# Two layers of a hybrid trunk on one core: a planner's table of durations refitted, selector products replaced by lane shuffles, the inverse's products cut in 64-wide quarters, and the last layer's queries for half of the tokens

## The chip, the cores and the metric

The kernel runs on one core of one Trainium2 chip. The metric is the device time of one execution in microseconds. The chip's engines are named as in the profile: PE (matrix), PEld (its weight loads), DVE (vector), ACT (scalar), POOL (GpSimd), and SP, which here only issues transfers.

## What is computed

Two layers run over 256 latent tokens and 256 context tokens of width 1024. In each, a projection feeds three mixers (a long convolution, a gated delta rule in chunks, and attention); their outputs are gated, summed and projected, and a mixture of 16 experts with two of them chosen for each token follows. The last layer needs its output for the latent tokens alone. Cut to what matters here:

```python
def gated_delta_chunked(q, k, v, g, beta, s0):
    ...
    m = jnp.where(strict, jnp.einsum('nbhid,nbhjd->nbhij', kb, kc) * gamma, 0.0)
    t_inv = lax.linalg.triangular_solve(eye + m, ...)     # (I + M)^-1 of each chunk and head
    u = t_inv @ (vc * bc[..., None])
    w = t_inv @ (kb * jnp.exp(gc)[..., None])
    a_intra = jnp.einsum('nbhid,nbhjd->nbhij', qc, kc) * gamma
    ...
def trunk_layer(x, cx, ..., update_ctx):
    ...
    o_c, s_f, s_b = gdn_bidir(gdn_features(qkv_c, ...), s_zero, s_zero)   # context first: state only
    o_l, _, _ = gdn_bidir(gdn_features(qkv_l, ...), s_f, s_b)             # then the latents
```

In the last layer `update_ctx` is false, so the queries of the context tokens lead to no output.

## The kernel before

All fp32 products that carry the accuracy are made as three fp32r products of a high and a low part (`mm3`, `split_block`): for each block of weights ACT writes the rounded part (CAST) and DVE the rest (TENSOR_TENSOR to fp32r).

**Order.** The program is written once, instruction by instruction, by a planner, and every engine runs its own list in that order. Dense work is a list of *items* (`layer`, `run`): each loads weights by SP, splits them ahead of time (`prep_ahead`), runs 24 or so matmuls on PE and evicts. An item is named after its matrix: `k0`, `q0`, `v0`, `z0` for the delta rule's inputs, `uq` for attention's queries, `gatehy`, `gatemla`, `gategdn` and `proj...` for gates and branch projections, `woutt` for the output projection, `up` and `down` for experts. Beside them run *streams*, which are Python generators: `gdn_pair` for two heads of the delta rule, `attend`, `hy_conv`, `filters`, `route` and others. After every piece of an item (6 or 12 matmuls) `tick` asks which stream is ready, and writes that stream's next step into the lists. "Ready" is the word of the class `Plan` (`enter`, line 252): it keeps a clock for each engine and adds a duration for each instruction from a table of formulas. Nothing of it runs on the chip; it only fixes the order. Where a step stands too early in PE's list, everything behind it waits.

**The delta rule's inverse.** `gdn_system` (line 1056) handles two heads, two directions and two chunks at once, eight 128x128 lower triangles. It is called for the context (base 2) and for the latents (base 0), for two head pairs and two layers: 8 calls, here called systems. In a system, the eight 16x16 blocks on each diagonal are packed in a tile `X16` and inverted by back substitution on DVE (15 steps of a multiply and a reduce). Each step needs one row of every block on all 16 partitions of the block. Before, 16 products with a 0/1 matrix `rsel` spread these rows (PE), and four copies by ACT evict them into `B`. Then blocks of 16 are merged to 32 and 32 to 64: for n = 16 and 32 and both directions, N times U, a masked copy (COPY_PREDICATED on DVE) into V, then T times V and V times T, and two copies by ACT back to U and T. Each of these is four products of 128x128 by 128x128. A last 64-wide step makes the two results, which `gdn_scan` uses.

**Memory.** Work tiles come from 45 pages of 4 KB a partition (`NPAGE`, `Arena`), and `rsel` takes 8 KB a partition (`late_setup`).

**Around the output projection**, `rows` (called in `woutt00` of layer 0 and `woutt02` of layer 1) issues transfers of the residual rows and modulation rows from ACT's queue; the splits of later `woutt` weights that the planner put behind them on ACT come after them.

Of the kernel before, what the change touches and what calls it, by code (L numbers as in the profile page):

```python
# [17 lines left out]
F32 = mybir.dt.float32  # L18
# [4 lines left out]
AF = mybir.ActivationFunctionType  # L23
OP = mybir.AluOpType
# [6 lines left out]
L = 2  # L31
# [3 lines left out]
C_HY, C_QKV, C_Z, C_AB, C_CQ, C_CKV, C_KR, C_GATE = 0, 1536, 3072, 3584, 3600, 4368, 4624, 4656  # L35
# [1 line left out]
FF = 512  # L37
CAP = (128, 96)
BIG = 1 << 20
NPAGE = 45  # L40


def _constants():
# [183 lines left out]
class Plan:  # L227
# [4 lines left out]

    def __init__(self):
        self.clk = dict.fromkeys(("tensor", "vector", "scalar", "gpsimd", "sync"), 0.0)
        self.dma = self.hw = 0.0
# [18 lines left out]
    def enter(self, eng, op, a, k):  # L254
# [4 lines left out]
        outs, ins = aps[:1], aps[1:]  # L259
# [3 lines left out]
        t = self.clk[eng]  # L263
        for q in ik:
            t = max(t, self.done.get(q, 0.0))
# [6 lines left out]
        if "dma" in op:  # L272
            byte = 4 * max(math.prod(aps[0].shape), 1)
            if op.startswith("indirect"):
                byte = 4 * min(math.prod(x.shape) for x in aps[:2])
            if eng == "gpsimd":
                self.clk[eng] = t + 1040
                t += 2000
            else:
                self.clk[eng] = t + 50  # L280
                self.hw = max(self.hw, t) + 450
                t = min(self.hw, t + 2000)
            self.dma = max(self.dma, t) + byte / 360
            end = min(self.dma, t + 8000 + byte / 360) + 2000
            if eng == "sync":
                self.clk[eng] = max(self.clk[eng], self.dma - 9000)
        else:
            if eng == "tensor":
                if op == "transpose":
                    c = 0.84 * max(64, size(outs[0]))  # L290
                else:
                    m, w = size(ins[0]), size(outs[0])
                    if ins[0].dtype == F32R:
                        c = 0.417 * w if w >= 256 else 0.84 * w
                    else:
                        c = 1.67 * max(w, m)
                        c = c / 4 if m <= 32 and w > 128 else c / 2 if m <= 64 else c
                if t > self.clk[eng] + 3000:
                    self.warm = t + 4000
                if t < self.warm:  # L300
                    c *= 2
            elif eng == "vector":
                fast = op in ("tensor_scalar", "tensor_copy") and not ps
                c = 70 + (0.52 if fast else 1.04) * n + (61 if op in ("tensor_scalar", "scalar_tensor_tensor") and len(aps) > (2 if op == "tensor_scalar" else 3) else 0)
            elif eng == "scalar":
                fn = a[2] if op == "activation" else None
                if fn in (AF.Sin, AF.Exp, AF.Tanh) and (fn == AF.Sin) != self.sin:
                    self.sin = not self.sin
                    t += 1280
                c = (51 if ps else 93) + 0.834 * n + 93 * (len(aps) - 2)  # L310
            else:
                c = 100 + {"tensor_tensor": 2.15, "memset": 0.77}.get(op, 3.4) * n
            end = t + c
            self.clk[eng] = end
            end += 200 if eng == "tensor" else 130
# [45 lines left out]
class Trunk:  # L361
# [456 lines left out]
    def gdn_item(self, l, kind, h):  # L818

        nc = self.nc  # L820
        t = 4 * "qkv".index(kind) + h

        def post(b):
            o, th = self.M.get(), self.M.get()
            self.conv(b, o.f(), l, "gdn_conv_w", t, 512)
            nc.scalar.activation(th.f(), o.f(), AF.Tanh, scale=0.5)
            nc.vector.scalar_tensor_tensor(o.f(), th.f(), 1.0, o.f(), op0=OP.add, op1=OP.mult)
            th.free()
            self.g_in[kind, h] = o
        return self.win(l, C_QKV + 128 * t, 512, post, f"{kind}{h}")  # L830

    def abkr_item(self, l):

# [96 lines left out]
    def gdn_pair(self, l, hp):  # L930
# [5 lines left out]
        nc = self.nc  # L936
# [8 lines left out]

        for kind in "kqv":
            bs = []
            yield max(self.plan.when(self.g_in[kind, h].f()) for h in heads)
# [95 lines left out]
    def gdn_system(self, l, hp, base, fm, tm, sys):  # L1044
# [51 lines left out]
        R = self.rsel  # L1096
# [12 lines left out]
        if want_o:  # L1109
            mI = self.c("maskI").rearrange("p (d x) -> p d x", d=2)  # L1110
            for d in range(2):
# [1 line left out]
            self.unbank(bQ)  # L1113
            g_.tensor_tensor(AT.f(), AT.f(), E.f(), op=OP.mult)
        E.free()
        Bv = [x.f().rearrange("p (k u j) -> p k u j", k=8, u=8) for x in B]
        for j in range(14, -1, -1):
            n = 16 - j
            if j >= 8:
# [24 lines left out]
            self.unbank(b)  # L1144
        X16.free()

        lm = self.c("lm").rearrange("p (n x) -> p n x", n=2).bitcast(U32)
        for i, n in enumerate((16, 32)):
            for d in range(2):
                yield self.plan.when(U[d].f())  # L1150
                b = self.bank()
                for u in range(4):
                    t_.matmul(b[:, 128 * u:128 * u + 128], N.f(128, 512 * d + 128 * u), U[d].f(128, 128 * u), start=True, stop=True)
                v.copy_predicated(u4(V[n, d].f()), m4(lm[:, i]), u4(b))
                self.unbank(b)
            for d in range(2):
                yield self.plan.when(V[n, d].f())
                b, b2 = self.bank(), self.bank()
                for u in range(4):
                    t_.matmul(b[:, 128 * u:128 * u + 128], T[d].f(128, 128 * u), V[n, d].f(128, 128 * u), start=True, stop=True)  # L1160
                for u in range(4):
                    t_.matmul(b2[:, 128 * u:128 * u + 128], V[n, d].f(128, 128 * u), T[d].f(128, 128 * u), start=True, stop=True)
# [1273 lines left out]
    def late_setup(self):  # L2436
# [7 lines left out]
        self.rsel = self.sb.tile([128, 16, 128], F32, name="rsel")  # L2444
        nc.scalar.dma_start(out=self.rsel.rearrange("p k x -> p (k x)"), in_=a["dft"][:, 2048:4096])
# [120 lines left out]
```

## Time and profile before

| | us |
|---|---|
| three timed runs | 2143.42, 2138.56, 2142.91 |
| median | 2142.91 |
| profiled execution, its own time | 2147.72 |
| its span, first to last instruction | 2146.0 |
| PE busy | 1919.7 (89%) |
| DVE, ACT, POOL busy | 1273.9, 872.5, 343.7 |

Times of the trace are from the span's start. Mixing of layer 0 takes some 50 to 785 us, its output projection and routing to 893, its experts to 1194; layer 1 mixes from 1248 to 1771, and its experts run from 1840 to 2109. A matmul of fp32 is recorded twice (two passes), one of fp32r once; since matmuls overlap, the spacing of many in a row tells their cost, not the mean length of one. Nearly all instructions carry line 210, the planner's recorder, so groups are told apart by tiles and shapes: `pg` is a page, `bank` a PSUM bank, `cst` a table of constants.

### The profile page before, as it was taken

The page shows a single profiled execution, that of the slowest core. Times are in us where ns is not written, and L with a number is a line of the kernel's source. Part 1 is how long each engine was busy: PE and PEld are TensorE (multiplying, and loading weights), DVE is VectorE, ACT ScalarE, POOL GpSimd, SP SyncE. Part 2 cuts the span into 40 slices and gives each one's busy share as a digit, 9 for nine tenths or more (in the row PEclk, how much of TensorE's full clock was granted, in tenths as well). Part 3 has the DMA queues.
Part 4 walks back from the last instruction along what each step waited for, and adds up shares of the span by engine and source line. Part 5 has one row for each costly group of instructions (what it writes and reads, how often), then busy time and mean ns, then how long its engine had stood idle before and what let it go on. Part 6 is the DMA issues. An engine that isn't in the chain of part 4 may idle for free. (4 is left out here: it accounts for less than half of the span.)

```text
span 2146.0 us, 31293 instructions
## 1 busy us (share of the span) xinstructions
PE 1919.7 (89%) x11901; PEld 1438.5 (67%) x11902; DVE 1273.9 (59%) x2487; ACT 872.5 (41%) x1445; POOL 343.7 (16%) x318
## 2 busy tenths in 40 slices
PE   4999999999999978799999399988999996899993
PEld 1777887777778857688777277877787884433330
DVE  3665757555466557899988576666766655311113
ACT  3442334444433423388778344433454342010101
POOL 1210222000133004311110211220011212110002
PEclk9999999999999998899999699999999997899996
DMA  9725223312533264699996647413214349799961
GB/s 332 228 89 175 67 57 94 89 50 79 157 99 82 94 242 174 230 362 383 381 359 218 201 176 258 116 40 89 70 54 118 109 140 370 251 382 390 386 264 67
DMA packets 295751, 403.62 MB, mean 188 GB/s; under 512 B 43956, under 2 KB 185786, under 8 KB 295464
## 3 DMA queue, kind: packets, MB, share of 16 engines
q1 hardware_dynamic: 271512, 360.38, 50.0%
q10 hardware_dynamic: 13040, 21.33, 2.8%
q0 software_dynamic: 11040, 19.81, 2.7%
q8 instruction: 96, 1.57, 0.3%
q14 instruction: 63, 0.52, 0.1%
HBM read 394.56 MB, written 23.20 MB: 195 GB/s over the span
## 5 line engine op out<-in xcount | busy, mean ns | idle before, releaser
L210 PE MATMUL bank<-pg,pg 128*128 128x512 f32 (+5 forms) x9958 | 1704.5, 407 | 66.3 <-ACT pg L210 36.5
L210 PEld LDWEIGHTS bank<-pg,pg 128*128 128x128 f32 (+3 forms) x9958 | 1252.0, 173 | 466.6 <-issue 202.5
L210 DVE TENSOR_TENSOR pg<-pg,pg 128x1024 fp32r<-128x1024 f32 (+12 forms) x698 | 607.7, 901 | 205.1 <-ACT pg L210 195.7
L210 ACT CAST pg<-pg 128x1024 fp32r<-128x1024 f32 (+3 forms) x460 | 429.0, 965 | 248.9 <-DVE pg L210 151.5
L210 ACT COPY pg<-bank 128x512 f32<-128x512 f32 (+4 forms) x382 | 185.2, 507 | 372.3 <-PE bank L210 341.6
L210 POOL TENSOR_TENSOR pg<-pg,pg 128x1024 f32<-128x1024 f32 (+3 forms) x77 | 134.7, 1754 | 494.1 <-DVE pg L210 291.6
L210 PE MATMUL bank<-cst,pg 128*128 128x128 f32 (+3 forms) x935 | 143.1, 290 | 78.3 <-DVE pg L210 48.8
L210 PEld LDWEIGHTS bank<-cst,pg 128*128 128x128 f32 (+1 forms) x935 | 118.4, 160 | 131.4 <-issue 55.1
L210 ACT ACTIVATE pg<-bank 128x512 f32<-128x512 f32 (+1 forms) x116 | 61.1, 534 | 196.7 <-PE bank L210 190.8
L210 ACT ACTIVATE pg<-pg 128x512 f32<-128x512 f32 (+4 forms) x71 | 50.0, 710 | 139.3 <-DVE pg L210 121.0
L210 POOL DMA_INDIRECT yd<-pg,t_vi x28 | 28.3, 1012 | 480.3 <-ACT pg L210 244.3
L210 DVE SCALAR_TENSOR_TENSOR pg<-bank,vec,pg 128x510 f32<-128x510 f32 (+3 forms) x112 | 75.4, 676 | 46.6 <-ACT pg L210 44.7
L210 DVE TENSOR_TENSOR pg<-bank,pg 128x512 fp32r<-128x512 f32 (+4 forms) x120 | 69.8, 597 | 50.5 <-ACT pg L210 34.7
L210 DVE SCALAR_TENSOR_TENSOR pg<-pg,bank 128x512 f32<-128x512 f32 (+1 forms) x92 | 54.0, 601 | 76.1 <-ACT pg L210 67.6
L210 POOL TENSOR_TENSOR pg<-pg 128x512 f32<-128x512 f32 (+1 forms) x18 | 18.5, 1034 | 458.6 <-ACT pg L210 272.6
L210 DVE COPY pg<-bank 128x512 f32<-128x512 f32 x24 | 16.6, 692 | 113.6 <-PE bank L210 111.6
L210 DVE TENSOR_TENSOR pg<-pg,bank 128x512 f32<-128x512 f32 (+1 forms) x44 | 27.0, 613 | 73.4 <-PE bank L210 71.0
L210 ACT ACTIVATE pg<-bank,vec 128x512 f32<-128x512 f32 (+3 forms) x64 | 42.2, 659 | 64.0 <-PE bank L210 57.0
L210 ACT CAST pg<-bank 128x512 fp32r<-128x512 f32 (+1 forms) x72 | 35.8, 521 | 74.7 <-PE bank L210 68.4
L210 ACT ACTIVATE pg<-bank,t_amx,t_asq 128x512 f32<-128x512 f32 (+1 forms) x48 | 34.0, 708 | 78.8 <-DVE t_amx L210 78.8
L210 PE MATMUL bank<-pg,sc 128*32 128x512 f32 x384 | 54.6, 627 | 1.0 <-DMA pg<-in_w_ada_dram 1.0
L210 DVE TENSOR_TENSOR pg<-bank,cst 32x256 f32<-32x256 f32 (+1 forms) x56 | 28.5, 518 | 29.2 <-PE bank L210 25.5
(250 smaller groups left out, 841.8 us busy)
## 6 DMA issues: line engine op xcount, KB each, us to landing
pg<-in_moe_w_dram SPq DMA_DIRECT2D x384, 512.0 KB
pg<-in_w_in_dram SPq DMA_DIRECT2D x120, 512.0 KB
pg<-in_w_ada_dram SPq DMA_DIRECT2D x96, 512.0 KB
pg<-in_w_out_dram SPq DMA_DIRECT2D x24, 512.0 KB
pg<-modd ACTq DMA_DIRECT2D x12, 512.0 KB
pg<-yd SPq DMA_DIRECT2D x12, 512.0 KB
pg<-in_mla_w_uq_dram SPq DMA_DIRECT2D x16, 288.0 KB
pg<-gcd POOLq DMA_DIRECT2D x16, 256.0 KB, 4.0
```

The source lines that it names most:

```text
L210: return f(*a, **k)
```

## The change

Four edits. (1) The formulas of `Plan.enter` get other numbers, and each issuing engine gets a transfer clock of its own. (2) The products with `rsel` and their copies go; 16 STREAM_SHUFFLE instructions on DVE spread the rows within groups of 32 partitions, row k over the k+1 columns that are used. `rsel` goes, and `NPAGE` rises to 47. (3) The three products of each merge step are made for the two 64x64 quarters on the diagonal alone, 8 calls of 64x64 by 64x64 where there were 4 of 128; masked copy and evictions are split by halves of the partitions. (4) In layer 1 the four `q` items work on 256 tokens where they had 512.

```diff
-            if eng == "gpsimd":
-                self.clk[eng] = t + 1040
-                t += 2000
-            else:
-                self.clk[eng] = t + 50
-                self.hw = max(self.hw, t) + 450
-                t = min(self.hw, t + 2000)
...
+            self.clk[eng] = t + {"sync": 50, "scalar": 330}.get(eng, 1040 if far else 700)
+            self.dma[eng] = max(self.dma.get(eng, 0.0), t + 2000) + byte / 385
...
-                        c = 0.417 * w if w >= 256 else 0.84 * w
+                        c = max(111, 14 + 0.417 * w)
...
+        nt = 512 if kind != "q" or l < L - 1 else 256
...
-        for q in range(4):
-            b = self.bank()
-            for k in range(4):
-                t_.matmul(b[:, 128 * k:128 * k + 128], R[:, 4 * q + k, :], X16.f(128, 256), start=True, stop=True)
-            nc.scalar.copy(B[q // 2].f(512, 512 * (q % 2)), b)
-            self.unbank(b)
+        for k in range(15, -1, -1):
+            v.stream_shuffle(Bv[k // 8][:, k % 8, :, :k + 1], C[:, :, :k + 1], [16 * (i // 16) + k for i in range(32)])
+            if k == 8:
+                yield
...
+        halves = (0, 64)
+        quad = lambda x, o: u4(x)[o:o + 64, :, o:o + 64]
...
+        def prod(b, A, a0, B, b0):
+            for u in range(4):
+                for o in halves:
+                    t_.matmul(b[o:o + 64, 128 * u + o:128 * u + o + 64], A.f(64, a0 + 128 * u + o)[o:o + 64], B.f(64, b0 + 128 * u + o)[o:o + 64], start=True, stop=True)
...
-                v.copy_predicated(u4(V[n, d].f()), m4(lm[:, i]), u4(b))
+                prod(b, N, 512 * d, U[d], 0)
+                for o in halves:
+                    v.copy_predicated(quad(V[n, d].f(), o), m4(lm[:, i])[o:o + 64, :, o:o + 64], quad(b, o))
...
-                nc.scalar.copy(U[d].f(), b)
-                nc.scalar.copy(T[d].f(), b2)
+                for o in halves:
+                    nc.scalar.copy(quad(U[d].f(), o), quad(b, o))
+                    nc.scalar.copy(quad(T[d].f(), o), quad(b2, o))
```

The counts of whole program: PE loses 128 products with `rsel`, 384 of 128x128 and 96 of 512 columns become 768 of 64x64 and 96 of 256; DVE gains 128 shuffles and 32 masked copies (32 become 64); ACT trades 96 copies of 128x512 for 128 of 64x4x64.

Most rows stand in another place than before. Three places matter later. The first is DVE's list in the last system of layer 1 (`pg_1740` is its X16, `pg_1744` and `pg_1745` its B). Before, PE had this part:

```order
L210 MATMUL bank_66<-pg_1641_12446,pg_1668_12827 128x128
L210 MATMUL bank_66<-pg_1637_12326,pg_1668_12827 128x128
L210 MATMUL bank_70<-pg_1700_13234,rsel 128x128 x4
L210 MATMUL bank_67<-pg_1700_13234,rsel 128x128 x4
L210 MATMUL bank_63<-pg_1700_13234,rsel 128x128 x4
L210 MATMUL bank_65<-pg_1700_13234,rsel 128x128 x4
L210 MATMUL bank_64<-pg_1725_13514,pg_1677_12972 128x128 x2
```

Now DVE has it:

```order
L210 STREAM_SHUFFLE pg_1744_14240<-pg_1740_14141 128x8x4
L210 STREAM_SHUFFLE pg_1744_14240<-pg_1740_14141 128x8x3
L210 STREAM_SHUFFLE pg_1744_14240<-pg_1740_14141 128x8x2
L210 STREAM_SHUFFLE pg_1744_14240<-pg_1740_14141 128x8
L210 TENSOR_TENSOR pg_1742_14147<-bank_63,cst_72 128x512 x2
L210 TENSOR_TENSOR pg_1740_14141<-pg_1740_14141,pg_1745_14241 128x8x2
L210 TENSOR_REDUCE pg_1740_14141<-pg_1740_14141 128x8
```

The spreading of rows left PE and ACT, and stands on DVE directly ahead of the substitution.

The second place is PE's list at the end of layer 1's mixing, where the gates of the delta rule (`gategdn`, 128x256) are the last dense items that need nothing of it. Before, the last 64-wide products of the last system stood between the first of these items:

```order
L210 MATMUL bank_68<-pg_1677_12972,pg_1728_13569 64x64 x4
L210 MATMUL bank_68<-pg_1745_13900,pg_1728_13569 64x64 x4
L210 MATMUL bank_70<-pg_1386_9807,pg_1752_13942 128x256 x2
L210 MATMUL bank_70<-pg_1386_9807,pg_1753_13943 128x256
L210 MATMUL bank_70<-pg_1389_9823,pg_1752_13942 128x256 x2
L210 MATMUL bank_70<-pg_1389_9823,pg_1753_13943 128x256
L210 MATMUL bank_70<-pg_1390_9832,pg_1752_13942 128x256 x2
L210 MATMUL bank_70<-pg_1390_9832,pg_1753_13943 128x256
L210 MATMUL bank_70<-pg_1391_9841,pg_1752_13942 128x256 x2
L210 MATMUL bank_70<-pg_1391_9841,pg_1753_13943 128x256
L210 MATMUL bank_67<-pg_1700_13234,pg_1505_10897 64x64 x4
L210 MATMUL bank_63<-pg_1675_12924,pg_1700_13234 64x64 x4
```

Now the merge of that system begins behind the last of them, `gategdn7`:

```order
L210 MATMUL bank_69<-pg_1394_10092,pg_1766_14471 128x256 x2
L210 MATMUL bank_69<-pg_1394_10092,pg_1767_14472 128x256
L210 MATMUL bank_69<-pg_1395_10101,pg_1766_14471 128x256 x2
L210 MATMUL bank_69<-pg_1395_10101,pg_1767_14472 128x256
L210 MATMUL bank_68<-cst_71,pg_1774_14572 128x128 x4
L210 MATMUL bank_70<-cst_71,pg_1775_14589 128x128 x4
L210 MATMUL bank_65<-pg_1775_14589,pg_1739_14132 64x64 x8
L210 MATMUL bank_67<-pg_1776_14590,pg_1739_14132 64x64 x8
L210 MATMUL bank_63<-pg_1776_14590,pg_1774_14572 64x64 x8
L210 MATMUL bank_64<-pg_1774_14572,pg_1776_14590 64x64 x8
```

From there to `projgdn0`, 160 calls of the system and of its scan follow each other with no dense item between them. Before, all eight `gategdn` items and half of `projmla3` lay between the same steps.

The third place is ACT's list ahead of `rows` in layer 0: the casts of 128x1024 are splits of `woutt` weights, those of 128x512 split merged outputs. Before, one stood there:

```order
L210 CAST pg_539_5799<-pg_518_5571 128x1024
L210 CAST pg_541_5805<-pg_366_3540 128x512
L210 CAST pg_542_5810<-pg_370_3617 128x512
L210 CAST pg_544_5841<-pg_379_3742 128x512
L210 CAST pg_545_5846<-pg_380_3771 128x512
L210 DMA pg_551_5859<-in_x_dram 128x1024
```

Now three do (and one more was made before these rows):

```order
L210 CAST pg_544_5979<-pg_517_5791 128x1024
L210 CAST pg_546_6009<-pg_351_3487 128x512
L210 CAST pg_547_6014<-pg_351_3487 128x512
L210 CAST pg_550_6033<-pg_518_5793 128x1024
L210 CAST pg_552_6051<-pg_363_3688 128x512
L210 CAST pg_553_6056<-pg_92_541 128x512
L210 CAST pg_554_6071<-pg_533_5927 128x1024
L210 CAST pg_556_6089<-pg_376_3876 128x512
L210 CAST pg_557_6094<-pg_363_3688 128x512
L210 DMA pg_560_6101<-in_x_dram 128x1024
```

So `woutt02` and `woutt03` are split before the transfers are issued, where only `woutt00` and `woutt01` were.

## Rows read from the trace of the kernel before

**Rows 1.** The page, busy time of PE.

```profile
PE 1919.7 (89%) x11901; PEld 1438.5 (67%) x11902; DVE 1273.9 (59%) x2487; ACT 872.5 (41%) x1445; POOL 343.7 (16%) x318
```

**Rows 2.** Windows: layer 0's and layer 1's mixing, the latter's end, its projection.

```profile
core 0: us, PE busy (x) PEld busy (x) DVE busy (x) ACT busy (x) POOL busy (x), PEclk, DMA share, GB/s
100.00:785.00 685.00, 675.69 (x3752) 540.87 (x3751) 411.05 (x887) 276.10 (x509) 99.77 (x102) 0.99 0.34 98
1254.00:1705.00 451.00, 411.98 (x2905) 359.21 (x2903) 302.12 (x713) 194.43 (x381) 66.05 (x74) 0.94 0.36 104
1704.00:1758.40 54.40, 49.52 (x429) 48.16 (x429) 28.86 (x58) 21.98 (x39) 10.77 (x10) 0.99 0.46 155
1771.00:1840.00 69.00, 44.16 (x196) 36.02 (x197) 40.56 (x114) 13.93 (x27) 19.35 (x11) 0.70 0.89 331
```

**Rows 3.** PE by shape, whole span: the selector products.

```profile
L210 PE MATMUL bank<-pg,rsel 128*128 128x128 f32 x256 | 34.3, 299 | 4.6 <-DVE pg L210 4.6
```

**Rows 4.** PE in order of time, 154 to 160 us: one system's selector products.

```profile
155.88 3.74 PE L210 MATMUL bank<-pg,rsel 128*128 128x128 f32 x32
```

**Rows 5.** PE by shape, 1709 to 1719.6 us: products of the inverse, last system.

```profile
L210 PE MATMUL bank<-pg,pg 128*128 128x128 f32 x80 | 9.5, 278 | 0.0
```

**Rows 6.** PE by shape, 213.3 to 214.4 us: eight calls in one array quarter.

```profile
L210 PE MATMUL bank<-pg,pg 64*64 64x64 f32 x16 | 1.1, 221 | 0.0
```

**Rows 7.** PE by shape, 219.7 to 220.6 us: eight such calls in two quarters.

```profile
L210 PE MATMUL bank<-pg 64*64 64x64 f32 x8 | 0.7, 224 | 0.0
L210 PE MATMUL bank<-pg,pg 64*64 64x64 f32 x8 | 0.7, 224 | 0.0
```

**Rows 8.** PE in order of time, 213 to 221 us: their end.

```profile
220.25 0.45 PE L210 MATMUL bank<-pg 64*64 64x64 f32 x5
220.63 0.62 PE L210 MATMUL bank<-pg,pg 128*128 128x256 f32 x3
```

**Rows 9.** PE in order of time, layer 1: items of 512 and 256.

```profile
1260.11 5.78 PE L210 MATMUL bank<-pg,pg 128*128 128x512 f32 x24
1281.84 5.93 PE L210 MATMUL bank<-pg,pg 128*128 128x256 f32 x48
```

**Rows 10.** DVE by shape, whole span: copies of two sizes, and the masked copy.

```profile
L210 DVE COPY pg<-pg 128x48 f32<-128x48 f32 x64 | 8.1, 193 | 0.1
L210 DVE COPY pg<-bank 128x512 f32<-128x512 f32 x24 | 16.6, 692 | 113.6 <-PE bank L210 111.6 <-DMA pg<-in_moe_w_dram 2.0
L210 DVE COPY_PREDICATED pg<-cst,bank 128x512 f32<-128x512 uint32 x32 | 22.8, 729 | 22.7 <-PE bank L210 22.6
```

**Rows 11.** ACT by shape, whole span: evictions of the two sizes.

```profile
L210 ACT COPY pg<-bank 128x512 f32<-128x512 f32 x220 | 126.6, 588 | 303.1 <-PE bank L210 288.0 <-issue 7.0 <-DVE pg L210 4.6
L210 ACT COPY pg<-bank 64x256 f32<-64x256 f32 x24 | 8.7, 366 | 12.6 <-PE bank L210 12.4
```

**Rows 12.** PE by shape, 1704 to 1757.6 us: end of layer 1's mixing.

```profile
L210 PE MATMUL bank<-pg,pg 128*128 128x256 f32 x216 | 28.1, 285 | 0.2 <-DVE pg L210 0.2
```

**Rows 13.** PE in order of time: where that stretch begins and ends.

```profile
1703.95 1.26 PE L210 MATMUL bank<-cst,pg 128*128 128x128 f32 x8 [1.67 <-DVE pg L210]
...
1757.61 1.11 PE L210 MATMUL bank<-cst,pg 128*128 128x128 f32 x4 [4.61 <-POOL pg L210]
```

**Rows 14.** DVE and POOL in order of time: the last steps before it.

```profile
1748.78 0.42 DVE L210 TENSOR_TENSOR pg<-pg,bank 128x256 f32<-128x256 f32 x1 [4.18 <-PE bank L210]
...
1755.69 1.87 POOL L210 TENSOR_TENSOR pg<-pg,t_ors 128x512 f32<-128x512 f32 x1 [3.66 <-DVE t_ors L210]
```

**Rows 15.** PE, then ACT, in order of time: layer 0's projection.

```profile
806.11 0.80 PE L210 MATMUL bank<-pg,pg 128*128 128x512 f32 x1 [15.47 <-ACT pg L210]
...
800.15 4.82 ACTq L210 DMA_DIRECT2D pg<-modd  x6
805.01 5.78 ACT L210 CAST pg<-pg 128x1024 fp32r<-128x1024 f32 x6 [11.17 <-DMA pg<-in_ctx_dram]
```

**Rows 16.** PE in order of time: layer 0's first gathered rows.

```profile
899.94 1.35 PE L210 MATMUL bank<-cst,pg 128*128 128x128 f32 x8 [2.08 <-DMA pg<-h2d,t_gi]
```

More of the change, by code (lines that the diff above doesn't have):

```diff
@@ L39 @@
 BIG = 1 << 20
-NPAGE = 45
+NPAGE = 47
 def _constants():
@@ L275, in enter @@
                 byte = 4 * min(math.prod(x.shape) for x in aps[:2])
-            if eng == "gpsimd":
-                self.clk[eng] = t + 1040
-                t += 2000
-            else:
-                self.clk[eng] = t + 50
-                self.hw = max(self.hw, t) + 450
-                t = min(self.hw, t + 2000)
-            self.dma = max(self.dma, t) + byte / 360
-            end = min(self.dma, t + 8000 + byte / 360) + 2000
+            far = op.startswith("indirect")
+            self.clk[eng] = t + {"sync": 50, "scalar": 330}.get(eng, 1040 if far else 700)
+            self.dma[eng] = max(self.dma.get(eng, 0.0), t + 2000) + byte / 385
+            end = self.dma[eng] + (2500 if far else 0)
             if eng == "sync":
-                self.clk[eng] = max(self.clk[eng], self.dma - 9000)
+                self.clk[eng] = max(self.clk[eng], end - 9000)
         else:
@@ L293, in enter @@
                     if ins[0].dtype == F32R:
-                        c = 0.417 * w if w >= 256 else 0.84 * w
-                    else:
-                        c = 1.67 * max(w, m)
-                        c = c / 4 if m <= 32 and w > 128 else c / 2 if m <= 64 else c
+                        c = max(111, 14 + 0.417 * w)
+                    elif m <= 32 and w > 128:
+                        c = 0.42 * w
+                    elif m <= 64:
+                        c = 0.84 * w if w > 64 else 74 if ins[0].shape[0] <= 64 else 116
+                    else:
+                        c = 2 * max(4 + 0.84 * m, 38 + 0.835 * w)
                 if t > self.clk[eng] + 3000:
@@ L821, in gdn_item @@
         t = 4 * "qkv".index(kind) + h
+        nt = 512 if kind != "q" or l < L - 1 else 256
         def post(b):
             o, th = self.M.get(), self.M.get()
-            self.conv(b, o.f(), l, "gdn_conv_w", t, 512)
-            nc.scalar.activation(th.f(), o.f(), AF.Tanh, scale=0.5)
-            nc.vector.scalar_tensor_tensor(o.f(), th.f(), 1.0, o.f(), op0=OP.add, op1=OP.mult)
+            self.conv(b[:, :nt], o.f(nt), l, "gdn_conv_w", t, nt)
+            nc.scalar.activation(th.f(nt), o.f(nt), AF.Tanh, scale=0.5)
+            nc.vector.scalar_tensor_tensor(o.f(nt), th.f(nt), 1.0, o.f(nt), op0=OP.add, op1=OP.mult)
             th.free()
             self.g_in[kind, h] = o
-        return self.win(l, C_QKV + 128 * t, 512, post, f"{kind}{h}")
+        return self.win(l, C_QKV + 128 * t, nt, post, f"{kind}{h}")
     def abkr_item(self, l):
@@ L947, in gdn_pair @@
             bs = []
-            yield max(self.plan.when(self.g_in[kind, h].f()) for h in heads)
+            yield max(self.plan.when(self.g_in[kind, h].f(128 * nq if kind == "q" else 512)) for h in heads)
             for j, h in enumerate(heads):
@@ L1102, in gdn_system @@
                 t_.matmul(bQ[:, 128 * i:128 * i + 128], fm["k", h].f()[:, tok(c)], fm["q", h].f()[:, tok(c)], start=True, stop=True)
[L1103 to L1108 removed]
+        Bv = [x.f().rearrange("p (k u j) -> p k u j", k=8, u=8) for x in B]
+        for k in range(15, -1, -1):
+            v.stream_shuffle(Bv[k // 8][:, k % 8, :, :k + 1], C[:, :, :k + 1], [16 * (i // 16) + k for i in range(32)])
+            if k == 8:
+                yield
         if want_o:
@@ L1115, in gdn_system @@
         E.free()
-        Bv = [x.f().rearrange("p (k u j) -> p k u j", k=8, u=8) for x in B]
         for j in range(14, -1, -1):
@@ L1158, in gdn_system @@
                 b, b2 = self.bank(), self.bank()
[L1159 to L1162, printed above, removed]
-                nc.scalar.copy(U[d].f(), b)
-                nc.scalar.copy(T[d].f(), b2)
+                prod(b, T[d], 0, V[n, d], 0)
+                prod(b2, V[n, d], 0, T[d], 0)
+                for o in halves:
+                    nc.scalar.copy(quad(U[d].f(), o), quad(b, o))
+                    nc.scalar.copy(quad(T[d].f(), o), quad(b2, o))
                 self.unbank(b)
```

11 lines of the change are left out of this document (3 added, 8 removed).

## Prediction

> **What bounds the kernel now.** I read the page first: PE is busy 89% of the span [rows 1]. Next the windows: in layer 0's mixing PE works 675.7 of 685 us, in layer 1's 412.0 of 451, at its end 49.5 of 54.4, while DVE stays under 70% and the transfers under half [rows 2]. So mixing is bound by PE, and work taken from PE there is time, as long as some other item stands behind it; what PE waits for is a chain of hand-overs where no item does. Only in the projection of layer 1 (44.2 of 69 us, DMA share 0.89, granted clock 0.70) do the transfers set the pace. Then PE by shape and in order of time, for the cost of each kind of call that the change touches; last PE's gaps, for the places where order matters.
>
> The sum is made against the profiled execution, 2147.72 us (span 2146.0 and 1.7 around it), 0.22% above the median 2142.91. The forecast takes the same difference off the median. What a measurement can tell from no change is 0.3%, or 6.4 us: 2136.5 to 2149.3.
>
> **Selector products.** 128 calls of 128x128 go. One system has 16, in 32 records over 3.74 us, the last of which runs on for some 0.2 us [rows 4]: 0.112 us for each record, 0.224 for a call. The group has 256 records, 8 systems [rows 3]. All stand in stretches where PE is the bound: -128 x 0.224 = **-28.7**.
>
> **Queries of layer 1.** An item of 24 matmuls with 512 columns takes 5.78 us; two items of 256 columns took 5.93, so 2.97 for one [rows 9]. Four items: 4 x (5.78 - 2.97) = **-11.2**.
>
> **Products of the inverse.** 384 calls of 128x128 at 0.224 (the stretch of 80 records, 9.5 us busy, gives 0.238 [rows 5]; I take the lower) are 86 us. In their place come 768 calls of 64x64. Eight in one quarter of the array are 16 records in 1.1 us, about 0.117 a call with the tail off [rows 6]; eight that alternate between two quarters take 0.7, some 0.06 a call [rows 7]. The change alternates the two diagonal quarters in its innermost loop, so I take 0.062: 47.6 us, -38.4. Against it speaks the change of shape: after the last 64-wide call starts at about 220.48, the next 128-wide one starts at 220.63, 0.15 later where the spacing was 0.06 [rows 8], so 0.09 each way. Runs of 64-wide calls rise from 16 to 39 in PE's list: 23 x 0.19 = +4.4. Together **-34**. [...]
>
> **The end of layer 1's mixing.** The stretch from the last system's transposes to the scan's last ones takes 53.7 us (1703.95 to 1757.61 [rows 13]), of which 28.1 are dense matmuls of 256 columns [rows 12]; PE then waits only 4.61 [rows 13], for the normalisation, which runs from DVE's 1748.78 over POOL's 1755.69 [rows 14]. In the new list nearly all dense items stand ahead of the merge, and the 160 calls after `gategdn7` have no cover. How long the chain is alone, no row shows. It can't be under 53.7 - 28.1 = 25.6 (the other PE work and the old waits), less the 34/8 = 4.2 saved above, nor over 53.7. In between: PE's own work 49.5 - 28.1 - 4.2 = 17; some fourteen hand-overs to DVE or ACT (transposes, twice masked copy and eviction, the 64-wide step, the scan's two chunks) at 0.7 (eviction 0.59, masked copy 0.73 [rows 10, 11]) = 10; and the 8.8 from 1748.78 to 1757.61. I take 36, nearer the lower end because it adds up the steps. PE idles 36 - 17 = 19 where it idled 4.6: **+15** (bounds +1 and +32).
>
> **Other systems.** Elsewhere the list has three runs of 40 to 64 calls of a system with no dense piece between (the first pair in both layers). Some 13 hand-overs of 0.7 to 1.2 us: **+12** (0, if order lets earlier work reach over, to 34, where the whole saving of the products is waited away).
>
> **Layer 0's end of mixing.** The scan's last transposes stand behind `gategdn7` now: between 0 and the 8.8 of the same chain [rows 14], **+3**.
>
> **Output projection.** In layer 0 PE waits 15.47 us at 806.11 for ACT, which first had to issue (4.82 at 800.15) and then waited 11.17 for a transfer before its next split [rows 15]. Two more `woutt` items are split ahead of those transfers, and PE has 2 x 2.9 us (an item's half of 12 matmuls with 512 columns, half of 5.78) that it can do meanwhile: -5.8; in layer 1 one more, with 256 columns, -1.5. **-7.3**. What is late next is the transfer itself; if it is also issued later, this is nothing.
>
> **Experts.** The first gathered rows come at 899.94 after 2.08 of waiting for them [rows 16]. They stand two pieces earlier in the new list, so the wait grows: **+3** (0 to 5.8, two pieces of 2.9).
>
> **Clock.** PE's granted clock is 0.99 where it is busy, 0.70 in the projection where it works 44 of 69 us [rows 2]. In the bare chain 17 us of work could cost up to twice that, 17; I take **+4**.
>
> **DVE, ACT, POOL.** 16 shuffles of 8 to 128 elements a system, 68 on average. No row has one. The nearest is the COPY of 128x48, 0.193 long and 8.1/64 = 0.127 apart; the copy of 512 elements from a bank takes 0.692 [rows 10]. I take 0.16, below 0.127 being unlikely and 0.69 the upper bound: 128 x 0.16 = 20 us over eight systems, 2.6 in each. It lies beside dense items (DVE is idle 40% of layer 0's mixing and 33% of layer 1's [rows 2]), while ACT loses 32 copies of 0.59: **0**. ACT's other trade, 96 copies of 0.59 for 128 of about 0.37 [rows 11], and the masked copies, 32 of 0.73 for 64 of about 0.4, are nothing either: ACT is 40% and 43% busy there [rows 2]. If the cover of dense items fails, as at layer 1's end, the shuffles of that one system are still done before it. Two pages more only loosen waits. [...]
>
> **Sum.** -28.7 - 11.2 - 34 + 15 + 12 + 3 - 7.3 + 3 + 4 = **-44**. The profile would be 2103.5, the median 2142.9 - 44 = **2099**.
>
> **Rivals.**
> A. *The spread becomes the wait* (slower). Each shuffle carries a selector and may cost more than a copy; the substitution can't start before them, the merge not before it, and DVE's list holds the splits of dense weights behind them. It decides where the extra DVE time has no cover: above 0.16 + 44/128 = 0.50 us a shuffle the gain is gone. At 0.69 the loss is 128 x 0.53 = 68: about **2167**. For it: the row of 0.69, and DVE at 67% in layer 1. Against: the small copies of 0.127. Chance 0.13.
> B. *The inverse is bound by its hand-overs*, not by PE: the 34 of the products are waited for instead, **2133**. For: each merge step has a masked copy and two evictions behind it, and now twice as many of them. Against: PE's 1.4% of idle in layer 0, where dense items fill every gap. Chance 0.14.
> C. *The quarters don't run side by side* (the change doesn't do what it says): 768 x 0.117 = 90 in place of 47.6, +42, **2141**. Rows 7 speak against it. Chance 0.06.
> D. *The refitted numbers also fill idle time elsewhere*: layer 1's mixing leaves 39 us idle on PE [rows 2]; half of it, -20, gives **2079**. For: almost every row moves, and 39 us is the largest idle sum in mixing. Against: the moved dense work at its end is covered in the sum already. Chance 0.19.
> The forecast's own case, 2085 to 2115, has 0.48.
>
> **How the numbers follow.** The range leaves out A and the far edge of D: it runs from 2065 (D with the tail at its lower bound, 2079 - 14) to 2145 (C, with the shape changes on top). Faster by over 0.3%: the forecast, D, two thirds of B: 0.76. Within: C and the rest of B: 0.11. Slower: A: 0.13.
>
> **What would show it.** The selector group is gone; 64x64 records spaced about 0.03 each in runs; `q` items of layer 1 at 3 us; PE's busy time down some 75 us, to about 1845. In the windows layer 0's mixing ends some 25 us earlier; the end of layer 1's mixing shows PE idle for about 19 us, with DVE and ACT as releasers and a lower granted clock. The gap at the output projection of layer 0 is near 10. Shuffles last 0.15 to 0.25 and PE waits for none. I am wrong if shuffles are above 0.5, if 64-wide calls are spaced 0.117, or if the idle time of mixing rises by over 50.

## Result and profile after

The changed kernel takes 2117.6 us (median of 4 runs, 2112.6 to 2123.5) where the one before takes 2143.2. The ratio is 0.9886, with a 95% interval of 0.9857 to 0.9916: 25 us faster, and some 19 us slower than the forecast of 2099. The profiled execution took 2112.6 with a span of 2110.9, so it is the fastest of its kernel, while that of before (2147.7) lies over its median; the two spans differ by 35 us, the medians by 25. The stages below add up to the 35, so they overstate the change by some 10 us, and no row tells in which stage. The page's line of busy time answers to [rows 1]: PE has 66 us less to do, and idles 31 us more.

```profile
PE 1853.4 (88%) x12413; PEld 1368.1 (65%) x12414; DVE 1296.4 (61%) x2775; ACT 855.6 (41%) x1477; POOL 338.4 (16%) x318
```

The view of windows, cut where the first matmul of a stage stands on PE (mixing of layer 0; its projection and routing; experts; the border; mixing of layer 1; projection and routing; experts), first for after:

```profile
core 0: us, PE busy (x) PEld busy (x) DVE busy (x) ACT busy (x) POOL busy (x), PEclk, DMA share, GB/s
50.00:781.10 731.10, 696.09 (x4202) 542.55 (x4201) 464.04 (x1112) 292.55 (x561) 114.58 (x114) 0.98 0.37 112
781.10:872.30 91.20, 70.60 (x372) 59.17 (x372) 69.98 (x158) 26.83 (x45) 39.44 (x19) 0.89 0.72 259
872.30:1162.80 290.50, 286.32 (x1343) 236.22 (x1339) 270.76 (x284) 233.75 (x285) 34.25 (x30) 0.99 0.87 325
1162.80:1218.00 55.20, 15.88 (x67) 10.84 (x66) 33.30 (x50) 20.20 (x27) 15.89 (x9) 0.66 0.93 290
1218.00:1727.60 509.60, 447.69 (x3702) 390.49 (x3702) 356.15 (x940) 219.20 (x450) 72.45 (x84) 0.93 0.40 114
1727.60:1796.70 69.10, 41.71 (x211) 34.43 (x213) 39.17 (x111) 12.57 (x25) 18.61 (x11) 0.73 0.89 330
1796.70:2074.00 277.30, 271.24 (x2461) 87.72 (x2450) 33.77 (x60) 27.67 (x47) 22.15 (x22) 0.99 0.84 311
```

and the same stages before (columns as above):

```profile
50.00:785.00 735.00, 722.92 (x3950) 579.85 (x3951) 444.35 (x964) 297.00 (x541) 112.30 (x114) 0.98 0.36 108
785.00:893.30 108.30, 74.56 (x373) 61.75 (x371) 77.78 (x164) 29.82 (x49) 41.92 (x19) 0.81 0.64 235
893.30:1194.30 301.00, 292.81 (x1341) 234.75 (x1337) 270.67 (x282) 236.50 (x284) 34.06 (x30) 0.99 0.87 318
1194.30:1248.40 54.10, 15.26 (x68) 10.22 (x67) 33.03 (x50) 20.21 (x27) 15.92 (x9) 0.68 0.94 295
1248.40:1771.40 523.00, 479.11 (x3444) 423.68 (x3444) 343.12 (x794) 223.85 (x432) 76.82 (x84) 0.95 0.37 110
1771.40:1840.20 68.80, 43.95 (x215) 35.82 (x214) 40.19 (x113) 13.93 (x27) 19.35 (x11) 0.70 0.89 330
1840.20:2109.00 268.80, 268.56 (x2455) 87.53 (x2443) 33.97 (x61) 27.60 (x47) 22.22 (x22) 1.00 0.87 323
```

| stage | before | after | difference | forecast |
|---|---|---|---|---|
| mixing, layer 0 | 735.0 | 731.1 | -3.9 | about -25 |
| projection and routing, layer 0 | 108.3 | 91.2 | -17.1 | -5.8 |
| experts, layer 0 | 301.0 | 290.5 | -10.5 | +3 |
| border | 54.1 | 55.2 | +1.1 | 0 |
| mixing, layer 1 | 523.0 | 509.6 | -13.4 | about -15 |
| projection and routing, layer 1 | 68.8 | 69.1 | +0.3 | -1.5 |
| experts, layer 1, with the end | 268.8 | 277.3 | +8.5 | 0 |

So the time came from other places than forecast. Layer 0's mixing, from which PE lost 27 us of work (722.9 to 696.1), gave 4: the rest became idle time. The projection and the experts of layer 0, whose work is the same, gave 28.

Two parts of that are plain in the rows. On PE in order of time, the waits of the two projections and of the first gathered rows of each layer are now:

```profile
797.86 0.79 PE L210 MATMUL bank<-pg,pg 128*128 128x512 f32 x1 [5.67 <-ACT pg L210]
...
878.15 1.92 PE L210 MATMUL bank<-cst,pg 128*128 128x128 f32 x8 [4.18 <-DMA pg<-h2d,t_gi]
...
1746.54 0.80 PE L210 MATMUL bank<-pg,pg 128*128 128x512 f32 x1 [11.88 <-ACT pg L210]
...
1804.67 1.97 PE L210 MATMUL bank<-cst,pg 128*128 128x128 f32 x8 [6.06 <-DMA pg<-h2d,t_gi]
```

The first answers to the 15.47 of [rows 15], the second to the 2.08 of [rows 16]. Layer 1's gathered rows cost 6.06, where PE waited for none before:

```profile
1850.61 1.09 PE L210 MATMUL bank<-cst,pg 128*128 128x128 f32 x8
```

The place in the list that was forecast at +3 in layer 0 exists twice, and the forecast priced one.

In the second part of layer 0's experts, PE by line, before (1050 to 1194 us) and after (1030 to 1163 us):

```profile
L210 PE MATMUL bank<-pg,pg 128*128 128x512 f32 x540 | 133.4, 400 | 6.0 <-DVE pg L210 5.0 <-ACT pg L210 0.9
```

```profile
L210 PE MATMUL bank<-pg,pg 128*128 128x512 f32 x543 | 127.9, 393 | 0.0
```

Splits on DVE and ACT were late there by 6.0 us, and are not now. The busy time of about as many calls also falls by 5.5 us, which no row explains. The refitted table alone makes these experts as short (below).

### The profile page after: what moved, and what is told of

Its sections match the earlier page's. It is cut to its first block, busy times and chain, and to the rows that moved or that the text cites. A ratio compares the mean times of both kernels' runs of the same rounds, so it can differ in the third digit from the quotient of the medians.

```text
span 2110.9 us, 32623 instructions
## 1 busy us (share of the span) xinstructions
PE 1853.4 (88%) x12413; PEld 1368.1 (65%) x12414; DVE 1296.4 (61%) x2775; ACT 855.6 (41%) x1477; POOL 338.4 (16%) x318
## 5 line engine op out<-in xcount | busy, mean ns | idle before, releaser
L210 PE MATMUL bank<-pg,pg 128*128 128x512 f32 (+7 forms) x10732 | 1663.8, 390 | 77.0 <-ACT pg L210 48.0
L210 PEld LDWEIGHTS bank<-pg,pg 128*128 128x128 f32 (+5 forms) x10732 | 1212.9, 167 | 476.8 <-issue 199.2
L210 DVE TENSOR_TENSOR pg<-pg,pg 128x1024 fp32r<-128x1024 f32 (+14 forms) x697 | 603.2, 897 | 169.3 <-ACT pg L210 158.8
L210 ACT COPY pg<-bank 128x512 f32<-128x512 f32 (+5 forms) x414 | 171.0, 444 | 346.0 <-PE bank L210 301.7
L210 PEld LDWEIGHTS bank<-cst,pg 128*128 128x128 f32 (+1 forms) x935 | 117.8, 159 | 156.7 <-issue 54.1
L210 POOL TENSOR_TENSOR pg<-pg,pg 128x512 f32<-128x512 f32 (+3 forms) x77 | 131.6, 1714 | 446.2 <-DVE pg L210 274.1
L210 DVE TENSOR_TENSOR pg<-bank,pg 128x512 fp32r<-128x512 f32 (+4 forms) x120 | 69.1, 596 | 30.7 <-ACT pg L210 23.5
L210 DVE TENSOR_REDUCE pg<-pg 128x128 f32<-128x1024 f32 (+15 forms) x128 | 43.1, 336 | 4.4
```

The source lines that it names most:

```text
L210: return f(*a, **k)
```

## Experiments

In all of them the kernel before, run beside them, took 2141 to 2143 us. Where a planner sets the order, an edit moves everything behind it; so the first set changes parts and lets the planner answer, and the second keeps every instruction at its place.

### Parts with the planner free

**The table alone.** Kernel before, with the new `Plan.enter`.

```diff
-            self.dma = max(self.dma, t) + byte / 360
+            self.dma[eng] = max(self.dma.get(eng, 0.0), t + 2000) + byte / 385
...
-                        c = 0.417 * w if w >= 256 else 0.84 * w
+                        c = max(111, 14 + 0.417 * w)
...
```

> The kernel before, with the refitted table of durations alone: no instruction is added or removed, only the order moves. If the gain of the change is the work taken from PE and the new order costs part of it (theory), this is 2135 to 2165, with the waits around layer 0's output projection and the long stretch of experts shorter, and more PE idle time in mixing. If the refit itself is where the gain comes from (rival), it is near the changed kernel: 2115 to 2125.

Measured: 2133.5, ratio 0.9961 (0.9947 to 0.9975), just under the theory's range and outside the rival's. Nothing is taken from PE, and 9 us are gained: layer 0's stage from `woutt00` to the experts falls from 108 to 91 us and its experts by about 10, as in the changed kernel, while mixing of both layers becomes longer (735 to 739, 523 to 529). So both gains come without any work taken from PE. The projection's is not the table's alone: in the three runs below that have the old table but another order (shuffles alone, quarters alone, all edits) that stage takes 91 to 93 us too, with PE's wait for ACT at 3.5 to 6.2 us for the 15.47, behind a mixing that is 18 to 42 us longer. The experts stay at 301 us in the first two of these runs and take 295 in the third.

**Shuffles alone** (old table, 45 pages).

```diff
-                t_.matmul(b[:, 128 * k:128 * k + 128], R[:, 4 * q + k, :], X16.f(128, 256), start=True, stop=True)
...
+            v.stream_shuffle(Bv[k // 8][:, k % 8, :, :k + 1], C[:, :, :k + 1], [16 * (i // 16) + k for i in range(32)])
...
```

> The kernel before, with the lane shuffles in place of the selector products alone (45 pages, old table). Theory: PE loses 128 x 0.224 = 28.7 us and DVE's shuffles are hidden: 2110 to 2120. Rival (the shuffles become the wait): no gain, 2140 or more.

Measured: 2154.3, ratio 1.0054 (1.0036 to 1.0072): slower by 12, as the rival had it.

**Quarter products alone**, with masked copies and evictions by halves.

```diff
-                    t_.matmul(b[:, 128 * u:128 * u + 128], N.f(128, 512 * d + 128 * u), U[d].f(128, 128 * u), start=True, stop=True)
+                prod(b, N, 512 * d, U[d], 0)
...
```

> The kernel before, with the 64-wide quarter products, masked copies and evictions alone. Theory: 34 us less on PE, 2105 to 2115. Rival (the merge is bound by its hand-overs): 2133 to 2143.

Measured: 2154.9, ratio 1.0061 (1.0044 to 1.0078): slower by 13, above both ranges.

**256-token queries alone.**

```diff
+        nt = 512 if kind != "q" or l < L - 1 else 256
```

> The kernel before, with the four query items of layer 1 on 256 tokens alone. Theory: 4 x 2.8 = 11 us less, 2130 to 2134. Rival (they cover something that is waited for anyway): 2140 or more.

Measured: 2148.1, ratio 1.0029 (1.0014 to 1.0044): slower by 6, as the rival had it.

**All edits with the old table** (47 pages).

```diff
-            self.dma[eng] = max(self.dma.get(eng, 0.0), t + 2000) + byte / 385
+            self.dma = max(self.dma, t) + byte / 360
...
```

> The changed kernel with the old table of durations (shuffles, quarters, 256 tokens and 47 pages stay). If the new order gives back part of what PE lost (theory), the old one keeps the sum of the parts better in mixing but has the long wait at layer 0's output projection: 2085 to 2115. If the refit is what gains (rival), 2125 to 2143.

Measured: 2172.3, ratio 1.0138 (1.0109 to 1.0167). Both theories' numbers are missed. Each edit that takes work from PE makes the kernel slower by itself under the old table, and together they do by 31. With the new table they give 2117.6. So the refit is worth 9 us to the old instructions and 55 to the new ones. That could be the order, or the edits' own cost, which these runs can't separate.

**Two pages less** in the changed kernel.

```diff
-NPAGE = 47
+NPAGE = 45
```

> The changed kernel with 45 pages. Layer 0's experts took 12 us less than before, which was not forecast. If the two pages do it (more weights under way), this is about 2130, with that stretch at 300 us again; if the order of the steps does it, 2112 to 2123 and 290 us.

Measured: 2131.9, ratio 0.9961 (0.9947 to 0.9975). The pages are worth 14 us, but not in the experts, which take as long as with 47: mixing does, 744 in place of 731 us in layer 0 and 522 in place of 510 in layer 1. I had costed them at nothing. Since the planner asks for free pages before it steps a stream, they move the order too.

### Parts with every instruction in its place

Here the planner goes on counting one form of the work, and the chip gets the other. Without this, the runs above can't be read.

**Wide products in the changed kernel.**

```diff
+                    self.plan.enter("tensor", "matmul", (b[o:o + 64, ...
...
+            self.plan.off = True
+                t_.matmul(b[:, 128 * u:128 * u + 128], A.f(128, a0 + 128 * u), B.f(128, b0 + 128 * u), start=True, stop=True)
+            self.plan.off = False
```

> The changed kernel, every instruction in the same place of every list, but with the merge's products 128 wide again (the planner still counts the 64-wide ones). If PE is the bound at the merges, 34 us more: 2147 to 2155. If the hand-overs bind there, the wider products lie in the waits: 2120 to 2130.

Measured: 2142.0, ratio 1.0000 (0.9988 to 1.0013): the quarters are worth 24 us in this order. It lies between the two expectations, nearer to PE as the bound. The page's line of busy time:

```profile
PE 1889.9 (88%) x11645; PEld 1409.8 (66%) x11646; DVE 1294.9 (60%) x2775; ACT 857.8 (40%) x1477; POOL 338.2 (16%) x318
```

PE has 36.5 us more to do than in the changed kernel (1853.4), and the kernel is 24 us longer, so some 12 of the work that the quarters save lie where PE would wait anyway. The masked copies and evictions are split in both kernels; what splitting costs is not in the 24.

**Each shuffle twice in the changed kernel.**

```diff
+            self.plan.off = True
+            v.stream_shuffle(Bv[k // 8][:, k % 8, :, :k + 1], C[:, :, :k + 1], [16 * (i // 16) + k for i in range(32)])
+            self.plan.off = False
```

> The changed kernel, same order, each lane shuffle issued twice: DVE gets 128 x 0.25 = 32 us more. If the shuffles are hidden, 2115 to 2123 as the changed kernel; if the shuffles are on the path, up to 2150, and what they cost now is of that size too.

Measured: 2142.6, ratio 1.0002 (0.9991 to 1.0014): 25 us slower, for 30 us more on DVE (1326.6 busy, 1296.4 in the changed kernel). The shuffles are not hidden.

**Shuffles in the order of before.** The planner counts the selector products and their copies, which aren't issued; the sixteen shuffles stand where they stood.

```diff
-                t_.matmul(b[:, 128 * k:128 * k + 128], R[:, 4 * q + k, :], X16.f(128, 256), start=True, stop=True)
+                self.plan.enter("tensor", "matmul", (b[:, 128 * k:128 * k + 128], R[:, 4 * q + k, :], X16.f(128, 256)), dict(start=True, stop=True))
...
+        self.plan.off = True
...
+            v.stream_shuffle(Bv[k // 8][:, k % 8, :, :k + 1], C[:, :, :k + 1], [16 * (i // 16) + k for i in range(32)])
+        self.plan.off = False
```

> The kernel before, with the planner still counting the selector products, so that every instruction keeps its place, and the shuffles issued where the products stood. With a new order the shuffles made the kernel 12 us slower. If the order did that (theory), the products' 28.7 us come off here: 2112 to 2125. If the shuffles themselves are on the path (rival), 2140 to 2155 again.

Measured: 2154.0, ratio 1.0054 (1.0035 to 1.0074). The theory that the order gives the gain back falls: with no instruction moved, the time is the same 2154 that the free planner made. The page's line:

```profile
PE 1895.7 (88%) x11645; PEld 1409.5 (66%) x11646; DVE 1300.7 (61%) x2743; ACT 855.7 (40%) x1413; POOL 344.1 (16%) x318
```

PE has 24 us less to do than before (1919.7; 28.7 by the spacing of the calls), DVE 27 more (1273.9), and the kernel takes 11 us more by the medians (the two profiled executions differ by 2.4 alone). So the shuffles and what they bring cost some 35 to 40 here.

One system shows where. PE in order of time, before, 590 to 626 us:

```profile
593.48 3.74 PE L210 MATMUL bank<-pg,rsel 128*128 128x128 f32 x32
...
616.59 0.66 PE L210 MATMUL bank<-cst,pg 128*128 128x128 f32 x4 [0.46 <-DVE pg L210]
```

and with the shuffles in the same order:

```profile
595.20 5.32 PE L210 MATMUL bank<-pg,pg 128*128 128x512 f32 x22 [0.53 <-DVE pg L210]
...
619.50 2.13 PE L210 MATMUL bank<-cst,pg 128*128 128x128 f32 x8 [5.58 <-DVE pg L210]
```

The selector's 3.74 us are gone, and the transposes behind the same three dense items, which started at 616.59 after a wait of 0.46, start at 619.50 after one of 5.58. DVE in order of time, the substitution's first steps and its last, before:

```profile
597.91 0.18 DVE L210 TENSOR_TENSOR pg<-pg,pg 128x16 f32<-128x16 f32 x1
...
598.32 2.35 DVE L210 TENSOR_TENSOR pg<-pg,pg 128x24 f32<-128x24 f32 x1
...
615.52 0.29 DVE L210 TENSOR_REDUCE pg<-pg 128x8 f32<-128x128 f32 x1
```

and with the shuffles:

```profile
600.91 0.17 DVE L210 TENSOR_TENSOR pg<-pg,pg 128x16 f32<-128x16 f32 x1
...
601.32 2.35 DVE L210 TENSOR_TENSOR pg<-pg,pg 128x24 f32<-128x24 f32 x1
...
618.43 0.29 DVE L210 TENSOR_REDUCE pg<-pg 128x8 f32<-128x128 f32 x1
```

The substitution takes 17.9 us before and 17.8 now, with under 1 us of idle time on DVE in either; it starts 3.0 us later. Of these, 2.4 are the sixteen shuffles ahead of it, and 0.6 is that DVE came to this system later (its last long reduce ahead of the shuffles starts at 589.15 before, at 589.72 now). So the gain of one system is taken back, with more, at its next step, because DVE has nothing to hide the shuffles behind. The multiply of 128x24 lasts 2.35 us in both, where it takes 0.20 alone (in the kernel before, at 248.47); it is looked at below.

**All edits in the order of before** (old table, 45 pages): quarters and 256 columns in the same way.

```diff
+            if self._plan.small:
+                a = tuple(half(x) for x in a)
             return f(*a, **k)
...
```

> The kernel before with all three edits in its own order: the planner counts the old instructions, the chip gets shuffles, quarter products and 256-token queries (old table, 45 pages). With the order left to the old table these edits gave 2172. Theory (the order gives the gain back): 2143 - 28.7 - 24 to 34 - 11 = 2070 to 2085. Rival (the work left PE, and what it covered is waited for in any order): 2125 to 2145.

Measured: 2137.5, ratio 0.9971 (0.9961 to 0.9982), in the rival's range. Against the run with shuffles alone, quarters and 256-token queries together are worth 16.5. The planner with the old table had made 2172 of the same edits, with two pages more: there the order did cost, some 35 us.

**All edits in the order that the new table makes for the old instructions** (45 pages): the kernel of the run above, with the diff of the table alone.

> The same on the order that the refitted table makes for the old instructions (45 pages); that order alone took 2133. Theory: 2060 to 2080, faster than both kernels. Rival: 2115 to 2135.

Measured: 2120.4, ratio 0.9902 (0.9878 to 0.9927): 13 us less than the same order with the old instructions. The rival's range, again.

### What is late on DVE

DVE in order of time in the changed kernel, 156 to 166 us: two of a system's shuffles, and the first steps of the substitution behind them.

```profile
158.91 0.01 DVE L210 LOAD_MASK_SELECT pg<-pg  x1
158.91 0.22 DVE L210 STREAM_SHUFFLE pg<-pg 128x64 f32<-128x64 f32 x1
...
159.05 0.23 DVE L210 STREAM_SHUFFLE pg<-pg 128x56 f32<-128x56 f32 x1
...
161.24 0.17 DVE L210 TENSOR_REDUCE pg<-pg 128x8 f32<-128x16 f32 x1
161.44 2.24 DVE L210 TENSOR_TENSOR pg<-pg,pg 128x24 f32<-128x24 f32 x1
163.72 0.18 DVE L210 TENSOR_REDUCE pg<-pg 128x8 f32<-128x24 f32 x1
163.93 0.21 DVE L210 TENSOR_TENSOR pg<-pg,pg 128x32 f32<-128x32 f32 x1
```

POOL at the same time:

```profile
161.23 2.40 POOL L210 TENSOR_TENSOR pg<-pg,pg 128x1024 f32<-128x1024 f32 x1 [0.81 <-DVE pg L210]
```

A shuffle follows the last by 0.14 here. Each has a LOAD_MASK_SELECT of 0.01 us ahead of it. The multiply of 128x24 takes 2.24 us, where its neighbour of 128x32 takes 0.21: it ends at 163.68, within 0.05 us of POOL's product of 128x1024, AT times E, which started just ahead of it at 161.23 and took 2.40. No row names POOL as what held it; that is read from the two ends. Six of the eight systems have such a product. Before, DVE waited for the selector's evictions while POOL made it: in three of the six the product fell into that wait nearly whole (the first multiply, 128x16, took 0.19, 0.27 and 0.44 us), in two it held the first multiply for part of its length (0.94 and 1.48 us), and in one, that of 598.32 above, it held the second for 2.35. With the shuffles in the same order all six are held for 2.2 to 2.35, some 8 us more in all. With the 19 of the shuffles this makes up the 27 by which DVE's busy time rose. The products with a bank as source and the shuffles, of which 24 ran beside POOL's products in the run of shuffles in the order of before, were not longer for it. In that run the seven shuffles from 157.43 on, beside POOL's product of 128x512 at 156.93, take 0.27 to 0.31 us, and the same seven from 597.31 on, beside none, 0.26 to 0.32; in the kernel before, the pair of products with a bank takes 1.28 at 157.39, beside POOL's product at 156.89, and 1.28 at 243.44, beside none.

The last run moves POOL's product, and the two mask products of DVE that it needs, ahead of the shuffles, in the kernel of 2120.4:

```diff
+            for d in range(2):
+                v.tensor_tensor(u4(AT.f(512, 512 * d)), u4(bQ), m4(mI[:, d]), op=OP.mult)
+            g_.tensor_tensor(AT.f(), AT.f(), E.f(), op=OP.mult)
...
         for k in range(15, -1, -1):
...
-            g_.tensor_tensor(AT.f(), AT.f(), E.f(), op=OP.mult)
```

> The previous kernel on the refitted order (2120), with one thing moved: the two mask products of the intra-chunk matrix (DVE, from a PSUM bank) and POOL's product of 128x1024 behind them stand ahead of the sixteen shuffles and no longer behind them; everything else keeps its place. In the runs so far DVE's second multiply of the substitution (128x24, 0.20 us alone) lasts 2.2 to 2.35 in the six systems in which POOL's product runs beside it, and no shuffle that ran beside POOL's work was longer. Theory (that stall holds up the transposes): six times 2.1 us come off DVE, the six multiplies are 0.2 again, and the kernel is 5 to 13 us faster: 2107 to 2115. Rival (POOL then stalls another instruction, or the masks wait for PE): 2117 to 2125.

Measured: 2103.0 (2098.5 to 2109.3), ratio 0.9810 (0.9785 to 0.9834). That is 17 us less than without the move, more than expected, and faster than both kernels. By the two ratios the move is worth 12 to 27 us, and the two profiled executions differ by 11, so the stall that was known, six times 2.1 us, may be all of it. The same system without the move, DVE, POOL and PE in order of time:

```profile
596.68 2.34 DVE L220 TENSOR_TENSOR pg<-pg,pg 128x24 f32<-128x24 f32 x1
...
596.56 2.40 POOL L220 TENSOR_TENSOR pg<-pg,pg 128x1024 f32<-128x1024 f32 x1 [2.68 <-issue]
...
612.17 1.72 PE L220 MATMUL bank<-cst,pg 128*128 128x128 f32 x8 [4.82 <-DVE pg L220]
```

and with it:

```profile
592.57 0.29 DVE L220 STREAM_SHUFFLE pg<-pg 128x96 f32<-128x96 f32 x1
...
594.18 0.34 DVE L220 TENSOR_TENSOR pg<-pg,pg 128x16 f32<-128x16 f32 x1
...
594.76 0.21 DVE L220 TENSOR_TENSOR pg<-pg,pg 128x24 f32<-128x24 f32 x1
...
592.07 2.41 POOL L220 TENSOR_TENSOR pg<-pg,pg 128x1024 f32<-128x1024 f32 x1 [0.26 <-PE bank L220]
...
607.10 1.26 PE L220 MATMUL bank<-cst,pg 128*128 128x128 f32 x8 [1.85 <-DVE pg L220]
```

The multiply of 128x24 is 0.21 again, the shuffle of 128x96 at 592.57, beside POOL's product, still takes 0.29, and PE waits 1.85 where it waited 4.82.

## Why the prediction came out as it did

- **The sum.** -44 was forecast, -25 measured: inside the range, faster as forecast, but outside the forecast's own case (2085 to 2115). Several terms were wrong, and partly cancel: the selector's was off by some 40 us, and gains that were not forecast, or not in full (the pages, layer 0's projection and experts), stand against it. That the total still lies in the range is in part luck.
- **Selector products, -28.7, with shuffles at 0.** This is the step that failed, and it is rival A by another price. The shuffles were sized well: 0.16 was taken, and sixteen take 2.4 us in all in the run of shuffles in the order of before (0.15 each), 19 over eight systems. By form on DVE in the changed kernel (the second number behind the bar is the mean in ns; they overlap):

```profile
L210 DVE STREAM_SHUFFLE pg<-pg 128x96 f32<-128x96 f32 x8 | 2.3, 292 | 0.0
L210 DVE STREAM_SHUFFLE pg<-pg 128x64 f32<-128x64 f32 x8 | 1.8, 224 | 0.0
L210 DVE STREAM_SHUFFLE pg<-pg 128x8 f32<-128x8 f32 x8 | 1.5, 194 | 0.0
```

  But "it lies beside dense items" was read from DVE's share of 60% over a window. At the substitution shown above DVE has next to no idle time, PE's transposes stand behind it, and what is added there is waited for. In the order of before the pair costs +11 where -28.7 was written; what it costs in the changed kernel's own order was not measured, but there a second set of shuffles cost 25. The rival's condition (0.50 us a shuffle) was wrong with it: the loss came at 0.15, and with a stall in the multiply behind the shuffles (2.24 us for 0.21), which no row of the shuffles shows.
- **Products, -34.** Right for PE: quarters run side by side at the price that was taken. The 48 records at 1685.76 (below) take 1.62 us with the last one running on for some 0.2, so 0.03 a record and 0.06 a call, and PE's busy time differs by 36.5 us between wide products and quarters in the changed order. In time, 24 came through. The 12 that are waited for are of the size of the +12 that I added for exposed merges, which these runs don't tell from other waits. In the order of before the quarters give, with the queries, 16.5, of 45 forecast; PE idles 30 us of layer 0's mixing there, where it idled 12.
- **The end of layer 1's mixing.** The chain alone was put at 36 us: by the rows that the forecast used it takes 34.5 (1678.73 to 1713.20). PE in order of time from the last system's transposes, and the window from `gategdn7`'s end to `projgdn0`:

```profile
1678.73 1.26 PE L210 MATMUL bank<-cst,pg 128*128 128x128 f32 x8 [0.90 <-DVE pg L210]
...
1682.45 2.97 PE L210 MATMUL bank<-pg,pg 64*64 64x64 f32 x80 [0.15 <-DVE pg L210]
1685.76 1.62 PE L210 MATMUL bank<-pg,pg 64*64 64x64 f32 x48 [0.34 <-ACT pg L210]
...
1713.20 1.12 PE L210 MATMUL bank<-cst,pg 128*128 128x128 f32 x4 [8.00 <-POOL pg L210]
```

```profile
1677.80:1714.30 36.50, 23.61 (x310) 21.36 (x310) 18.13 (x53) 13.39 (x33) 3.26 (x4) 0.82 0.31 102
```

  It answers to [rows 13]: the last wait is now 8.00 for the 4.61. PE's own work was put at 17 and is 23.6 in the window, at a granted clock of 0.82, so idle is 12.9 and not 19. If 0.18 of the 23.6 is the clock's, that is 4.2 us, the size of the +4; this is an estimate, and no run here separates it. For the forecast's "up to twice" the kernel before has these stretches: from 1789 to 1793 us PE is busy all the time at a granted clock of 0.50, with 9 records of 128x512, and from 812 to 816 us at 1.00, with 20. That this exposed chain is a loss is not shown, since mixing of layer 1 is shorter in this order (509.6) than in that of the kernel of 2120.4 (525.0).
- **Queries, -11.2.** Alone they don't gain. How much is left in place was not separated from the products.
- **Output projection, -7.3.** Layer 0's wait fell by 9.8, to 5.67; PE's time there fell as well, by 4, at a granted clock of 0.89 for 0.81. Right in place, too small in size. That the earlier splits are what does it was not tested alone. Layer 1's went the other way, 9.6 in two waits before to 11.88.
- **Experts.** +2.1 for the gathered rows against +3; the same step in layer 1 (+6.06, and 8.5 for the stage) was overlooked, and so was the order inside layer 0's experts (-10 from the first gathered rows on).
- **Two pages, 0.** They are worth 14 us in the changed kernel.
- **Rivals.** C is out (0.06 a call, not 0.117). B holds in part: of the 36.5 us that the quarters take from PE, 24 came through. D has no sign in the place that it named, since PE's idle time in layer 1's mixing rose from 43.9 to 61.9 us; but the new table did shorten another place, layer 0's projection and experts, and by more than the sum had.

What is left open: why the old table orders the new instructions worse by 35 us; which share of the gain is the queries'; what the shuffles cost in the changed kernel's own order.

## What to carry to other kernels

Before work is moved from the bound engine to one that is 60% busy, look at the second engine at that place, instruction by instruction: if what it does there is waited for next, the work is only moved down the path. Look also at which other engine's work used to fall into the wait that the move closes; here it was POOL's product, in part. Where a planner sets the order, hold the order to price an edit, and let the planner free to price the table: the two answers for all edits with the old table differed by 35 us here, more than the change was worth.

## What the runs showed of the hardware

DVE's multiply of two pages took 2.24 us, where its neighbour took 0.21, and ended with a POOL product that had started 0.21 ahead of it (changed kernel, 161.44), while shuffles beside such a product kept their time (128x96: 0.29 in the last run at 592.57, and 0.29 at 598.10, beside none, in the run of shuffles in the order of before). 64x64 calls that alternate between two quarters follow each other at 0.06 us (the 48 records at 1685.76 in the changed kernel), those in one quarter at about 0.12 [rows 6].
